# Dividing tiles 48 to 73 of a row maximum anew, and letting GpSimd find most of the last number-free rows

## Chip, cores, metric

One core of a Trainium2 chip. The metric is the device time of one execution in microseconds (us), as a median of several executions.

## The reference

```python
batch, seq, dim = 32, 2048, 2048
x = np.random.randn(batch, seq, dim).astype(np.float32)
x[np.random.rand(batch, seq, dim) < 0.1] = np.nan
return np.nanmax(x, axis=-1).astype(np.float32)     # 65536 rows of 2048; a row without numbers gives NaN
```

## The kernel before

Each of 128 partitions holds 512 rows. They are read in 74 tiles of 28 quarter rows (28Q; 1Q is 512 elements, the first tile has 4Q). Work on a tile goes through three engines: ScalarE reads the upper 16 bits of each float and writes a key in which NaN has become smaller than every number (a "read"); GpSimd, or for a part of the tile ScalarE, turns keys back into upper halves (a "write-back"); VectorE takes the maximum of each row. Each tile is described by its loads, its pieces for ScalarE's reads (a negative number is written back by ScalarE itself, a tuple is read at once and written back apart) and its reductions, all in Q:

```python
TILES = (
    [([4], [4], [4])]
    + [([28], [7, 9, 12], [16, 12])] * 7
    + [([28], [9, 12, -7], [8, 20])]
    ...                                   # this pair of lines six times: tiles 1 to 48; then 49 to 57; cut
    + [([28], [7, 9, 12], [12, 16])] * 3                    # tiles 58 to 60
    + [([28], [7, 9, 12], [16, 12])]                        # tile 61
    + [([19, 9], [12, (5, -7), 4], [12, 16])]               # tile 62
    ...                                                      # cut
    + [([5, 4, 4, 4, 3, 4, 4], [2, 3, 4, (1, -2), 2, 3, 3, 4, (-1, 3)], [4, 8, 4, 4, 4, 4])]
    + [([4, 4, 3, 2, 3, 4, 1, 2, 3, 2], [4, 4, 3, -2, 3, (3, -1), 3, (-1, 1), 2, -1], [4, 4, 4, 4, 4, 4, 4])]
)
GROUPS = [TILES[i : i + 15] for i in range(0, 60, 15)] + [TILES[60:]]
FLAGGED = (3, 4)                          # after these groups the number-free rows are found
...
                    for c in parts:
                        ...               # kp: this piece's keys, to: where they go; cut
                        if back:
                            e = act([e_key], out=to, in_=kp, func=ACT.Copy, bias=float(TOP), scale=-1.0)
                        else:
                            e = pool([e_key], out=to, in0=kp, scalar1=-1.0, scalar2=float(TOP), op0=ALU.mult, op1=ALU.add)
...
            e = dve(after, nc.vector.tensor_scalar, out=none, in0=acc, scalar1=NONE,
                    scalar2=float(0x00C00000), op0=ALU.is_equal, op1=ALU.mult)
            e = dve([e], nc.vector.tensor_tensor, out=bits, in0=bits, in1=none, op=ALU.bitwise_or)
```

A row without numbers comes out as one known value (NONE); the two last instructions find it and make NaN of it. For the last 98 rows of a partition they stand behind the very last reduction, and the store of those rows behind them.

## Time and profile before

| | before |
|---|---|
| median of 3 runs | 1253.81 us (1253.79 to 1254.08) |
| span of the profiled run | 1251.8 us |
| VectorE, ScalarE, GpSimd busy | 89%, 79%, 93% |
| HBM read | 536.87 MB, 429 GB/s over the span |
| read of the last bytes | all but stragglers by about 1242.1 us; last load landed 1242.66 us |
| last reduction ends | 1248.23 us |

The prediction shows the lines that carry this. DVE is VectorE, ACT ScalarE, POOL GpSimd, SPq the queue that issues loads and stores. In a chain of waits a line is start, length, engine and line of the kernel, "x9" is nine instructions in a row; "idle before <- releaser" in brackets, in a timeline, is how long the engine stood and what ended it. The reading of it: the read fills everything up to 1242, so the change can only touch the tail.

### The profile page before, as it was taken

The numbers are of one execution on the slowest core, as the hardware profiler recorded it, in microseconds if no ns is written. First come the engines' busy times: TensorE is split into PE (matmuls) and PEld (weight loads), VectorE is DVE, ScalarE is ACT, GpSimd is POOL, SyncE is SP. The second block draws the span as 40 slices with busy tenths as digits, with TensorE's granted clock in tenths as the row PEclk, the third lists the DMA queues.
The fourth block names the chain that finished last, engine by engine and source line by source line (L and its number), as shares of the span: only waits on it lengthen the run. The fifth ranks groups of instructions, "written<-read, shape, count | busy, mean of one in ns | idle before, by whom it ended". The sixth has DMA issues, their size and how long they took to land.

```text
span 1251.8 us, 872 instructions
## 1 busy us (share of the span) xinstructions
DVE 1110.5 (89%) x169; ACT 988.5 (79%) x271; POOL 1166.9 (93%) x239
## 2 busy tenths in 40 slices
DVE  0888989888889988898988888998888899999999
ACT  3777887778787877788777877787777878989997
POOL 2999989998999899998999899989999999999997
DMA  9999999999999999999999999999999999999997
GB/s 415 440 421 429 440 440 440 424 427 440 440 440 427 424 440 440 438 431 421 440 440 438 432 420 440 440 438 434 418 440 440 436 438 421 431 434 426 430 427 289
DMA packets 16279, 537.20 MB, mean 429 GB/s; under 512 B 2448, under 2 KB 2448, under 8 KB 3472
## 3 DMA queue, kind: packets, MB, share of 16 engines
q1 hardware_dynamic: 16272, 537.14, 99.3%
q14 instruction: 7, 0.06, 0.0%
HBM read 536.87 MB, written 0.26 MB: 429 GB/s over the span
## 4 chain that ended last, share of the span: by engine, by line
DVE 37%; DMA 35%; POOL 17%; ACT 10%; issue 1%; SPq 0%; DVEq 0%
DVE acc L194 37%; DMA xt<-in_x_dram 35%; POOL xt L190 17%; ACT kt L186 9%; ACT xt L186 1%; SPq L228 0%; DVE none L194 0%; DVEq L124 0%; SPq L384 0%; SPq L182 0%
## 5 line engine op out<-in xcount | busy, mean ns | idle before, releaser
L190 POOL TENSOR_SCALAR xt<-kt 128x3584 int16<-128x3584 uint16 (+8 forms) x235 | 1166.7, 4965 | 78.7 <-ACT kt L186 60.1
L194 DVE TENSOR_REDUCE acc<-xt 128x3 f32<-128x6144 f32 (+4 forms) x164 | 1108.8, 6807 | 137.1 <-POOL xt L190 127.7
L186 ACT ACTIVATE kt<-xt,scalars 128x3584 uint16<-128x3584 int16 (+9 forms) x248 | 936.0, 3812 | 255.8 <-DMA xt<-in_x_dram 237.9
L186 ACT ACTIVATE xt<-kt 128x3584 int16<-128x3584 uint16 (+4 forms) x21 | 53.5, 2545 | 0.7
L186 ACT ACT_TABLE_LOAD x1 | 1.3, 1283 | 0.9 <-SPq L182 0.9
L196 DVE MEMSET scalars<- 128x1 f32 x1 | 0.1, 59 | 1.0 <-SPq L182 1.0
L194 DVE TENSOR_SCALAR none<-acc 128x414 int32<-128x414 f32 (+1 forms) x2 | 0.9, 428 | 0.1
L194 DVE TENSOR_TENSOR acc<-acc,none 128x414 int32<-128x414 int32 (+1 forms) x2 | 0.8, 422 | 0.1
L370 POOL MEMSET const-float32-0.0<- 128x1 f32 x1 | 0.1, 99 | 0.2 <-issue 0.2
L186 ACT ACTIVATE scalars<-scalars 128x1 f32<-128x1 f32 x1 | 0.2, 202 | 0.0
L370 POOL MEMSET const-bfloat16-1.0<- 128x1 bf16 x1 | 0.1, 102 | 0.0
L370 POOL MEMSET const-uint8-127<- 128x1 uint8 x1 | 0.1, 102 | 0.0
L370 POOL MEMSET const-float32-1.0<- 128x1 f32 x1 | 0.1, 99 | 0.0
## 6 DMA issues: line engine op xcount, KB each, us to landing
xt<-in_x_dram SPq DMA_DIRECT2D x61, 7168.0 KB, 22.5
xt<-in_x_dram SPq DMA_DIRECT2D x12, 1024.0 KB, 27.5
xt<-in_x_dram SPq DMA_DIRECT2D x5, 2048.0 KB, 22.0
xt<-in_x_dram SPq DMA_DIRECT2D x2, 4864.0 KB, 18.9
xt<-in_x_dram SPq DMA_DIRECT2D x2, 3584.0 KB, 22.0
xt<-in_x_dram SPq DMA_DIRECT2D x3, 2304.0 KB, 20.4
xt<-in_x_dram SPq DMA_DIRECT2D x5, 1280.0 KB, 26.3
xt<-in_x_dram SPq DMA_DIRECT2D x1, 4608.0 KB, 18.5
```

What stands on the lines that cost most here:

```text
L186: return order.add("act", nc.scalar, lambda: nc.scalar.activation(**kw), deps)
L190: "pool", nc.gpsimd, lambda: nc.gpsimd.tensor_scalar(**kw), deps
L194: return order.add("dve", nc.vector, lambda: do(**kw), deps)
L196: e_top = order.add("dve", nc.vector, lambda: nc.vector.memset(top, EDGE), [])
L370: nc = _bacc.Bacc("TRN2", target_bir_lowering=False, num_devices=1)
```

## The change

Its intent is a shorter tail. First, VectorE's finding of the last rows shrinks from 98 rows to 7: the rows of tiles 60 to 72 become a group of their own, and GpSimd finds them behind its last piece. (The words of the change say two tiles; in the code one tile is left to VectorE.) The finding now multiplies by 0x00800000, and GpSimd adds the result to the bits where VectorE ORs it in; both still make a NaN of NONE. Second, tiles 48 to 73 are divided anew (51 and 56 stay as they were). Third, a write-back given as a float is held until ScalarE has issued its next read, unless it is the tile's last; so two are held, one in tile 72 and one in tile 73.

```diff
-    + [([28], [9, 12, -7], [8, 20])]                 # tile 48
-    ...
+    + [([28], [6, 10, 12], [16, 12])] * 3
+    ...                                               # tiles 51 to 60; cut
+    + [([28], [8, 11, 9], [8, 8, 12])]               # tile 61
+    + [([20, 8], [11, -6, 6, 5], [16, 12])]          # tile 62
+    ...                                               # cut
+    + [([5, 6, 5, 4, 4, 3, 1], [(-2, 3), 3, 3, (4, -1), 4, 4, -2.0, 2], [4, 4, 3, 1, 4, 4, 4, 4])]
+    + [([4, 4, 3, 2, 4, 2, 3, 3, 3], [2, 2, 4, (-2.0, 1), 2, 3, 3, (-1, 2), (1, -1, 1), 2, -1.0], [4, 4, 4, 4, 4, 4, 4])]
 )
-GROUPS = [TILES[i : i + 15] for i in range(0, 60, 15)] + [TILES[60:]]
-FLAGGED = (3, 4)
+GROUPS = [TILES[i : i + 15] for i in range(0, 60, 15)] + [TILES[60:73], TILES[73:]]
+FLAGGED = (3, 5)
+LATE = 4
...
+                    release()             # after the next read: write back what was held
                     for c in parts:
...
                         if back:
-                            e = act([e_key], out=to, in_=kp, func=ACT.Copy, ...)
+                            held.append((at - c, at, key, kp, e_key))
+                            if not wait or at == sum(loads) * Q:
+                                release()
...
+            if gi == len(GROUPS) - 1:
+                e = find("pool", nc.gpsimd, late_after, late_acc, late, ALU.add)
+                ready[LATE] = e
```

## The prediction

> **What bounds the kernel now.** I read the page first (busy shares, the forty slices), then the chain that ended last, then the operation groups by shape, then single engines and windows of 1 us near the end. Tiles are numbered from 0; every tile but the first is 28 quarter rows (28Q; a quarter is 512 elements) per partition, so 7 rows. The page:
>
> ```profile
> span 1251.8 us, 872 instructions
> DVE 1110.5 (89%) x169; ACT 988.5 (79%) x271; POOL 1166.9 (93%) x239
> DMA  9999999999999999999999999999999999999997
> GB/s 415 440 421 429 440 440 440 424 427 440 440 440 427 424 440 440 438 431 421 440 440 438 432 420 440 440 438 434 418 440 440 436 438 421 431 434 426 430 427 289
> ```
>
> No compute engine is full over the span, but DMA is full in every slice but the last: the kernel lives on one read of 536.87 MB. To be won are only the head and the tail behind the last load, and the change leaves the head alone. Windows of 1 us (stretch, length, busy us of VectorE, ScalarE, GpSimd, clock, DMA share, GB/s):
>
> ```profile
> 1240.00:1241.00 1.00, 1.00 (x1) 1.00 (x2) 1.00 (x1) 1.00 0.97 396
> 1241.00:1242.00 1.00, 1.00 (x2) 1.00 (x2) 0.69 (x2) 1.00 0.89 265
> 1242.00:1243.00 1.00, 1.00 (x1) 0.97 (x2) 1.00 (x1) 1.00 0.17 43
> 1243.00:1244.00 1.00, 1.00 (x2) 1.00 (x2) 0.92 (x2) 1.00 0.00 0
> ```
>
> The last load is in at about 1242.1. Behind it lie 9.7 us, 0.8% of the span. The chain from tile 61 on (start, us, what), cut to its two ends:
>
> ```profile
> 1037.96 3.29 ACT kt L186
> 1041.25 0.07 issue
> 1041.32 4.19 POOL xt L190
> 1045.51 0.08 issue
> 1045.59 5.34 POOL xt L190
> 1050.94 0.02 issue
> 1050.96 66.86 DVE acc L194 x9
> ...
> 1245.93 2.30 DVE acc L194
> 1248.23 0.02 issue
> 1248.25 0.27 DVE none L194
> 1248.53 0.02 issue
> 1248.55 0.26 DVE acc L194
> ```
>
> Tile 61 lands at 1037.96; ScalarE and GpSimd prepare its first 16Q; from 1050.96 VectorE never stops: 43 reductions of 91 rows in 197.3 us (to 1248.23). So the end of the tail is VectorE's, though not by much: the timeline of ScalarE shows that it, too, is full from 1229.93 on, and its last write-back starts at 1245.05 and takes 0.79, to 1245.84, just before VectorE's last reduction at 1245.93:
>
> ```profile
> 1243.29 1.73 ACT L186 ACTIVATE kt<-xt,scalars 128x1024 uint16<-128x1024 int16 x2
> 1245.05 0.79 ACT L186 ACTIVATE xt<-kt 128x512 int16<-128x512 uint16 x1
> ```
>
> **What the Trainium skill says.** ScalarE: Activation LUTs, section What ACT_TABLE_LOAD costs: an ACTIVATE with a pointer bias takes about 280 ns + 0.833 ns per element, and neighbours overlap by about 93 ns. The trace agrees for the reads (1536 elements: 1560 ns; reads of 3584 and 4608 elements, 3279 and 4122 ns apart, take 7.31 us together, 90 ns less). The write-backs are slower than that page has it (186 ns + 0.833 per element, 1465 ns at 1536, for immediate operands): 1929 ns here, which I use. GPSIMD Engine Reference, section 3.1: an add of two inputs takes about 2.6 cycles per element at 1.2 GHz, some 0.2 us for 91 elements (my estimate); no such instruction is in the trace. SBUF — State Buffer, section Who interferes with whom: tensor_reduce never contends with GpSimd on trn2. The trace agrees: one row takes 2274 to 2276 ns beside a busy GpSimd, and 2.30 us in the last with GpSimd idle. DMA: Bandwidth & Descriptors, section Where 436 GB/s comes from: a ceiling of 435 GB/s; the trace has 440 in many slices, so this read is at the ceiling and a new order of work can't hasten it.
>
> **The change part by part.**
>
> Landings. The same bytes are read in the same order. First loads of tiles 58 to 61 land 16.89 us apart (ScalarE's waits end at 987.30, 1004.18, 1021.07, 1037.96), and the queue was never dry, so tile 61 again lands at 1037.96 and the last load at about 1242.1. The pieces of the tail's loads are about as many as before, so I change nothing here.
>
> Start of VectorE's unbroken run. Durations by shape: ScalarE reads of 6Q, 8Q take 2.85, 3.70; GpSimd 6Q 3.62, 8Q 4.77, 9Q 5.34, 10Q 5.91, 11Q 6.48; about 0.08 between. Tile 60, now 6, 10, 12: its first 16Q are ready at 1021.07 + 2.85 + 0.07 + 3.62 + 0.08 + 5.91 = 1033.6, reduced by 1048.8 (15.15 for a tile). Tile 61, now 8, 11, 9 with reductions of 2, 2 and 3 rows: GpSimd ends the pieces at 1037.96 + 3.70 + 0.07 + 4.77 = 1046.5, 1053.06 and 1058.5. VectorE: 1048.8 to 1053.2, to 1057.6, waits 0.9, 1058.5 to 1065.1. Before, tile 61 was done at 1050.96 + 15.2 = 1066.15: 1.05 us gained.
>
> VectorE's work after it. From 2276 ns for one row and 8686 for four: (8686 - 2276)/3 = 2.137 us per row and 0.14 per instruction, of which about 0.08 overlaps with the one before (8.69 + 6.55 against 15.15 for a pair), leaving 0.06. Check on before: 91 x 2.137 + 43 x 0.06 = 197.0, measured 197.3. Tiles 62 to 73 had 41 reductions and get 52 (2, 3, 3, 2, 3, 3, 5, 5, 4, 7, 8, 7): 11 x 0.06 = 0.7 us more. New end of the last reduction: 1065.1 + 84 x 2.137 + 52 x 0.06 = 1247.7, if it never waits; before, 1248.2. Net gain about 0.4, allowing 0.1 us of idle time.
>
> ScalarE and GpSimd. Over tiles 61 to 73 write-backs rise from 15 of 44Q to 19 of 49Q. From the durations by shape I sum 197.7 us for ScalarE (194.6 before) and 191.6 for GpSimd (194.5 before), against 204.2 us from tile 61's landing to the last. ScalarE's 3.1 us go into waits (the view of waits gives it 8.1 us on reads and 1.7 on GpSimd from 1050 on before). The two pieces marked as held write back behind the next read: the gap of 0.03 between a read and its own write-back becomes an overlap of about 0.1, so 0.13 each, 0.3 us in all, already in that sum.
>
> Last tile on ScalarE. It can begin at about 1227.5, when its first 4Q are in (1225.03, seen at the end of a wait, plus 4 x 0.61). Eleven reads: 11 x 0.28 + 28 x 0.428 = 15.1; write-backs of 2, 1, 1 and 1Q: 1.35 + 3 x 0.78 = 3.7; overlaps less gaps -1.2: 17.6 us, to 1245.1, against 1245.84 before. The floor from the last landing is 1242.1 + 1.13 + 0.7 + 0.8 = 1244.7. So ScalarE frees the last row 0.7 us sooner, and that is no longer what holds the end: VectorE gets to it at 1247.7 - 2.28 = 1245.4.
>
> Finding the number-free rows. VectorE's two instructions shrink from 98 elements to 7 (the code leaves one tile, not two, to the last group). From 593 ns at 414 elements and 264 at 98: 1.04 ns each, so 91 fewer spare 2 x 0.095 = 0.19 us on the path. GpSimd's two instructions on 91 elements, an estimate of 0.3 us each from its fixed 0.2 us and the above, start when its last piece is done, about 1244.8, and end near 1245.5 beside VectorE's last reductions: hidden. One store more, ready about two us ahead of the last: hidden too. The last store's 3.5 KB should take the 1.7 us of the 49 KB one.
>
> Sum: 0.4 + 0.2 = 0.6 us off 1253.81: 1253.2.
>
> **The rivals.** First, new waits on VectorE: with 52 reductions cut to fit the pieces, each waits for one piece, and ScalarE is 3 us fuller. For it speaks that a walk by hand over tiles 62 to 67 leaves margins of only 0 to 2 us between a piece being ready and VectorE asking for it; against it, that a late piece in the middle is no loss unless VectorE ends later than ScalarE allows. It would cost 0.5 to 1.5 us: 1253.7 to 1254.7. Second, VectorE gains more and the last landing binds: 1244.8 + 0.1 + 2.28 + 0.35 = 1247.5 for the end of the finding against 1248.81 now, so 1252.5; nothing can go below this unless the read gets faster. For it speaks that ScalarE is so near it. Third, without the write-back of tile 48 on ScalarE (9, 12, -7 gave way to 6, 10, 12) twenty tiles run with 16.6 us of GpSimd work against 16.9 us of reading, and 16.7 where the slices show 440 GB/s. GpSimd could fall behind by some 0.1 us per tile there, but slices of 420 give it back, and the tiles from 49 to 61 ran so before. I give it under 0.5 us. Fourth, the finding on GpSimd or its store ends last: it has about 2 us of room, so it would have to take four times my estimate; then up to +1 us.
>
> **Range and chances.** The middle is 1253.2. Floor 1252.5, less 0.5 for another read rate: 1252.0. Above, waits of the first rival and a little of the third: 1254.6. A gain of 2% is 25 us, nearly three times all that lies behind the last load; a loss of 2% would need a new wait of about 1.8 us in each of the last 14 tiles, with nothing to absorb it. Faster 0.01, same 0.98, slower 0.01.
>
> **What would show it.** Right: DMA full until about 1242; VectorE's chain unbroken from about 1058.5; its last reduction ending near 1247.7; the last finding two instructions of about 0.17 us on 7 elements; ScalarE's last write-back done near 1245.1; GpSimd's two instructions over by 1246. Wrong: if VectorE shows idle time behind ScalarE or GpSimd between 1060 and 1245, if the reads end elsewhere than at 1242, or if the store of the 91 rows is what the end waits for.

## The result, and the profile after

The change takes 1253.68 us (median of 6 runs, 1253.59 to 1253.85) against 1253.89 us for the kernel before in the same rounds (6 runs, 1253.76 to 1254.15). The ratio is the mean time of one kernel's fast runs over that of the other's of the same rounds, so not quite the ratio of the medians: 0.9998, 95% interval 0.9985 to 1.0011. That is the same within 2%, and 0.2 us lower in the medians.

From the page of the changed kernel (its span is 1251.8 us, as before):

```profile
DVE 1110.9 (89%) x181; ACT 986.9 (79%) x273; POOL 1168.4 (93%) x242
DMA  9999999999999999999999999999999999999997
```

The DMA row is as before. The windows of 1 us show the bulk of the read ending where it did (264 and 53 GB/s in the two windows where before had 265 and 43), but stragglers of the last load land later: it was complete at 1243.20 instead of 1242.66.

```profile
1241.00:1242.00 1.00, 1.00 (x1) 1.00 (x2) 0.92 (x2) 1.00 0.88 264
1242.00:1243.00 1.00, 1.00 (x2) 1.00 (x1) 1.00 (x1) 1.00 0.19 53
```

The chain that ended last, cut to tile 61 and the last rows, without its "issue" lines of 0.02 to 0.08 us:

```profile
1038.12 8.60 ACT kt L187 x2
1046.79 6.48 POOL xt L191
1053.35 5.35 POOL xt L191
1058.72 6.55 DVE acc L195
...
1213.18 23.03 DMA xt<-in_x_dram
1236.24 1.58 ACT kt L187
1237.89 1.92 POOL xt L191
1239.84 2.01 DVE acc L195
...
1246.42 2.29 DVE acc L195
1248.74 0.18 DVE none L201
1248.94 0.16 DVE acc L215
```

Two things are to be seen. Tile 61 went as worked out: done at 1058.72 + 6.55 = 1065.27, 27.15 us after its landing, where before needed 28.15. But the chain no longer runs through VectorE alone: it goes back from the fourth-last reduction over GpSimd and ScalarE to a load of the last tile that landed at 1236.21, and the last reduction ends at 1248.71, not earlier than before but 0.48 us later. The timeline around it:

```profile
1233.78 1.15 ACT L187 ACTIVATE kt<-xt,scalars 128x1024 uint16<-128x1024 int16 x1 [0.33 <-DMA xt<-in_x_dram]
1237.89 8.42 POOL L191 TENSOR_SCALAR xt<-kt 128x1536 int16<-128x1536 uint16 x6 [0.95 <-ACT kt L187]
1239.84 8.87 DVE L195 TENSOR_REDUCE acc<-xt 128x1 f32<-128x2048 f32 x4 [0.50 <-POOL xt L191]
1245.54 0.77 ACT L187 ACTIVATE xt<-kt 128x512 int16<-128x512 uint16 x1
1246.40 0.55 POOL L201 TENSOR_SCALAR late<-acc 128x91 int32<-128x91 f32 x1
1247.03 0.34 POOL L215 TENSOR_TENSOR acc<-acc,late 128x91 int32<-128x91 int32 x1
```

GpSimd stood 0.95 us and VectorE 0.50 us behind that read of ScalarE's. The load itself left ScalarE idle for only 0.07 us, the load before it for 0.33 us (first line), so the chain's last step names the smaller of two waits for the read. ScalarE and GpSimd both end their last piece at 1246.31, and GpSimd's finding (0.55 and 0.34 us) is over at 1247.37, hidden.

Laid side by side, the two spans agree, in four terms: tile 61 landed 0.16 us later (1038.12 against 1037.96); from there to the end of the last reduction it took 210.59 instead of 210.27 us (+0.32); the finding on VectorE 0.39 instead of 0.58 (-0.19); and from there to the end of the span 2.70 instead of 2.97 us (-0.27), of which most is the last store: the one of 3.5 KB landed in 1.40 us, the one of 49 KB in 1.66. The sum is 0.02. So the finding and the small store gained about half a microsecond, and the new tail gave most of it back.

The second term is the steadier measure: the end of the last reduction less the landing of tile 61 (the moment at which ScalarE's wait for it ends). Times of whole runs of one kernel differ by up to 0.9 us, and over the traces tile 61 lands anywhere from 1037.92 to 1038.58 us, whichever kernel it is; this "tail length" of one kernel's traces agrees within 0.13 us.

### The profile page after: what moved, and what is told of

Same layout as the page of the kernel before. It is cut to its first block, busy times and chain, and to the rows that moved or that the text cites. A ratio compares the mean times of both kernels' runs of the same rounds, so it can differ in the third digit from the quotient of the medians.

```text
span 1251.8 us, 892 instructions
## 1 busy us (share of the span) xinstructions
DVE 1110.9 (89%) x181; ACT 986.9 (79%) x273; POOL 1168.4 (93%) x242
## 4 chain that ended last, share of the span: by engine, by line
DMA 36%; DVE 33%; POOL 19%; ACT 10%; SPq 1%; issue 1%; DVEq 0%
DMA xt<-in_x_dram 36%; DVE acc L195 33%; POOL xt L191 19%; ACT kt L187 9%; ACT xt L187 1%; SPq L253 1%; DVE none L201 0%; DVE acc L215 0%; SPq L411 0%; DVEq L124 0%; SPq L183 0%
## 5 line engine op out<-in xcount | busy, mean ns | idle before, releaser
L191 POOL TENSOR_SCALAR xt<-kt 128x3584 int16<-128x3584 uint16 (+11 forms) x236 | 1167.4, 4946 | 78.5 <-ACT kt L187 60.3
L187 ACT ACTIVATE xt<-kt 128x512 int16<-128x512 uint16 (+6 forms) x24 | 52.8, 2200 | 0.7
```

The source lines that it names most:

```text
L187: return order.add("act", nc.scalar, lambda: nc.scalar.activation(**kw), deps)
L191: "pool", nc.gpsimd, lambda: nc.gpsimd.tensor_scalar(**kw), deps
```

## The experiments

All were correct. "Before" is the kernel before in the same rounds. Medians are of 5 runs (4 where said), of before 9.

**Which half gained: the finding alone.** Before's tiles, the change's finding and its groups.

```diff
 # the change, with
-TILES = ...  # the change's
+TILES = ...  # before's
```

> The tiles of before with the new finding alone (13 tiles' rows on GpSimd, 7 rows on VectorE). Theory A (the two halves of the change pull apart: the finding gains, the tiles lose): the last reduction ends as before, near 1248.2; the finding takes 0.35 instead of 0.55 us; the small last store lands 0.3 us sooner than the 49 KB one; so about 0.5 us faster than before (1253.4) and 0.3 faster than the change. Theory B (the finding on GpSimd gains nothing, the 0.2 us are the tiles'): as before, 1253.9.

Measured: 1253.56 us, before 1253.93; ratio 0.9998 (0.9984 to 1.0012). The tail is before's to the hundredth, 1248.24 - 1037.97 = 210.27. Its last lines in the timeline:

```profile
1248.26 0.17 DVE L203 TENSOR_SCALAR none<-acc 128x7 int32<-128x7 f32 x1
1248.47 0.16 DVE L217 TENSOR_TENSOR acc<-acc,none 128x7 int32<-128x7 int32 x1
```

The expectation of Theory A is met in its direction (0.37 us below before, 0.5 expected; the change, in other rounds, was 0.21 below); the store's part did not show in this trace (1.7 us to landing). Repeated on another chip:

> The tiles of before with the new finding again, on another chip: 0.3 to 0.4 us below before if that gain is real, 210.27 us from tile 61's landing within 0.05, and the small last store 0.25 us quicker from its issue than the 49 KB one (the first trace of it did not show that).

Measured: 1253.52 us, before 1253.90 (ratio 0.9998, 0.9984 to 1.0012). Tail 210.18, 0.04 beyond what I allowed. The store landed in 1.54 us, 0.12 quicker than the large one and not 0.25. Twice 0.37 or 0.38 us below before in the median, so the gain is as steady as this measure allows, though the interval of the ratio does not part it from zero. No kernel is further below before; it was never run in the same rounds as the change, so that it beats the change rests on two comparisons with before. Measured in the traces from tile 61's landing to the end of the span, it gains 0.18 and 0.40 us.

**The other half: the tiles alone.** The change with before's finding of 98 rows on VectorE.

```diff
-GROUPS = [...] + [TILES[60:73], TILES[73:]]
+GROUPS = [...] + [TILES[60:]]
-FLAGGED = (3, 5)
+FLAGGED = (3, 4)
```

> The new tiles with the old finding (98 rows on VectorE at the end, one 49 KB store). Theory A: the last reduction ends at about 1248.7, 0.5 us later than before, and nothing makes it good: about 0.4 to 0.5 us slower than before, 1254.3. Theory B (the tiles are what gained): 0.2 us faster than before, 1253.7.

Measured: 1254.17 us, before 1253.93; ratio 1.0003 (0.999 to 1.0015). Tail 210.61. Theory A holds in its direction: the new tiles lose 0.2 to 0.3 us (0.4 to 0.5 expected).

**Tiles 48 to 60.** Before, with only these divided as in the change; and the counterpart, the change with before's tiles 0 to 60.

```diff
-    + [([28], [9, 12, -7], [8, 20])]
-    + [([28], [7, 9, 12], [16, 12])] * 4 ...
+    + [([28], [6, 10, 12], [16, 12])] * 3 ...        # tiles 48 to 60 only
```

> Before, with only tiles 48 to 60 divided as in the change (no write-back on ScalarE in tile 48). If GpSimd falls behind without that relief (third rival): first reduction of tile 61 later than 1051.0 and the end later by the same, up to 0.5 us. If not: tile 61 still waits for its landing, the last reduction ends at 1248.2 within 0.2, time as before within 0.2 us.

Measured: 1254.42 us, all five runs above 1254.2, before 1253.93; ratio 1.0004 (0.9991 to 1.0016). Tile 61 landed at 1038.40, 0.44 later than in the trace of before, and its first reduction was 13.26 us after that (1051.66; before 13.00), so 0.26 of lag; but the tail was 210.33, and the lag was gone at the end.

> Tiles 0 to 60 of before, tiles 61 to 73 and the finding of the change. The part alone of tiles 48 to 60 cost 0.49 us in the earlier run. Theory A (that cost is carried into the change): this is 0.3 to 0.5 us faster than the change. Theory B (the new tail absorbs GpSimd's lag, because tile 61 begins with a small reduction): same as the change within 0.15 us.

Measured: 1253.52 us (1253.47 to 1254.1), before 1253.67; ratio 1.0 (0.9987 to 1.0012). Tail 210.62. The change itself took 1253.52 in these rounds. Theory B: tiles 48 to 60 cost the change nothing. The 0.49 us of the first run do not lie in these tiles by its trace: it is 0.96 us longer than that of before, 0.44 by the later landing and 0.47 behind the finding, where the large store took 1.93 us to land instead of 1.66. Over all traces, kernels with before's tiles 48 to 60 land tile 61 at 1037.96, 1037.97, 1038.32, 1038.33 and 1038.58, those with the new ones at 1037.92 to 1038.58 (nine traces, median 1038.31): no difference. Why that one kernel was slow in all five runs stays open.

**The change again**.

> The change itself, word for word, on the chip of the other three. It gives what one chip and the next differ by, and a second trace: if the last loads and tile 61's landing move by 0.2 to 0.4 us between two traces of one kernel, differences of that size in a single trace are the read's, not the change's. Expected: 0.2 us below before, within 0.15; last reduction again held by ScalarE's read behind the fifth load of the last tile (0.4 to 0.6 us idle on VectorE near 1239.8).

Measured: 1253.52 us, before 1253.67; ratio 0.9999 (0.9985 to 1.0012): 0.15 us lower. The tail is 210.72 us, the same wait is there:

```profile
1239.78 8.86 DVE L195 TENSOR_REDUCE acc<-xt 128x1 f32<-128x2048 f32 x4 [0.48 <-POOL xt L191]
```

**Does VectorE's time bind?** The change, with the finding of the 91 rows moved from GpSimd to VectorE, between the last two tiles.

```diff
-FLAGGED = (3, 5)
-LATE = 4
+FLAGGED = (3, 4, 5)      # and no finding on GpSimd
```

> The change, but VectorE itself finds the rows of tiles 60 to 72 between the last reduction of tile 72 and the first of tile 73, about 0.55 us of VectorE time; GpSimd finds nothing. If VectorE's rows bind without a break (my prediction's reading): 0.5 us slower than the change. If VectorE is held by the last tile's landing and ScalarE (it waited 0.5 us at 1239.8 in the change's trace): the 0.55 us fall into that wait and the time is that of the change within 0.15 us.

Measured: 1253.78 us, before 1253.93; ratio 0.9999 (0.9986 to 1.0011). Tail 210.66, with 0.52 us more work on VectorE in the chain:

```profile
1232.88 0.27 DVE none L199
1233.16 0.25 DVE acc L213
```

VectorE's rows do not bind without a break: the work fell into its wait. It also shows that GpSimd was not needed for this gain; done on VectorE ahead of the last tile it cost no more, within the 0.13 us by which tails of one kernel differ.

**Is it the fifth load?** The chain of the change pointed to the load of quarters 13 to 17 in the last tile, of which ScalarE wants the first three. The change with that load cut smaller, and the write-back in front of the wait not held (two edits at once).

```diff
-    + [([4, 4, 3, 2, 4, 2, 3, 3, 3], [2, 2, 4, (-2.0, 1), 2, ...
+    + [([4, 4, 3, 2, 3, 3, 3, 3, 3], [2, 2, 4, (-2, 1), 2, ...
```

> The change, with the last tile's loads of 4 and 2 quarters cut as 3 and 3 and the first held write-back of that tile done at once. Theory A (the end hangs on the landing of the fifth load, which ScalarE's read of rows 13 to 16Q waits for; at 0.61 us per quarter it then comes 0.6 us sooner): last reduction 0.4 to 0.5 us sooner, time 0.4 us below the change. Theory B (VectorE's rows bind, the idle 0.5 us is given back elsewhere): no change within 0.15 us.

Measured: 1253.52 us, as the change in these rounds (1253.52); ratio to before 1.0 (0.9987 to 1.0012). Tail 210.56. The wait for that load is gone, but:

```profile
1237.23 11.34 DVE L195 TENSOR_REDUCE acc<-xt 128x1 f32<-128x2048 f32 x5 [0.19 <-POOL xt L191]
1239.15 1.57 ACT L187 ACTIVATE kt<-xt,scalars 128x1536 uint16<-128x1536 int16 x1 [0.20 <-DMA xt<-in_x_dram]
```

Five reductions follow one another, starting after a wait of 0.19, and end where they did; ScalarE waits for a later load, the seventh. Theory B's time came, but not for its reason that VectorE's rows bind. The chain that ended last in this run, cut:

```profile
1217.72 21.41 DMA xt<-in_x_dram
1239.15 1.58 ACT kt L187
...
1244.83 1.36 POOL xt L191
1246.28 2.30 DVE acc L195
```

From the landing of the seventh load, at 1239.13, ScalarE's four reads and three write-backs take 7.05 us; with them, at 1246.18, GpSimd's last piece is done, and VectorE's last reduction starts 0.10 us later, 2.38 us after the one before it instead of the usual 2.19. In the change the same path had the same length (1239.26 to 1246.31, the last reduction at 1246.42), and VectorE's own rows came out level with it. So the run relieved one of two equal paths, and removing the wait was worth at most 0.16 us.

**Holding write-backs.** The change with none held.

```diff
-4, 4, -2.0, 2]   ...   (-2.0, 1), 2, 3, 3   ...   2, -1.0]
+4, 4, -2, 2]     ...   (-2, 1), 2, 3, 3     ...   2, -1]
```

> The change without holding any write-back behind the next read. My prediction: two held write-backs are worth 0.13 us each on ScalarE, 0.3 us in all, so if ScalarE's work in the last tile sets the end this is 0.1 to 0.3 us slower. If the landing of the fifth load sets it, ScalarE waits for that load anyway (it had idle 0.33 us before it): same within 0.15 us.

Measured: 1253.96 us, before 1253.67, the change 1253.52; ratio 1.0002 (0.999 to 1.0015). Tail 211.07, 0.35 to 0.48 longer than the change's two.

```profile
1225.98 1.34 ACT L187 ACTIVATE xt<-kt 128x1024 int16<-128x1024 uint16 x1
1228.53 2.19 ACT L187 ACTIVATE kt<-xt,scalars 128x1024 uint16<-128x1024 int16 x2 [0.21 <-DMA xt<-in_x_dram]
1235.62 2.29 DVE L195 TENSOR_REDUCE acc<-xt 128x1 f32<-128x2048 f32 x1 [0.47 <-POOL xt L191]
1238.32 11.06 DVE L195 TENSOR_REDUCE acc<-xt 128x1 f32<-128x2048 f32 x5 [0.42 <-POOL xt L191]
```

The write-back at 1225.98 now stands ahead of the last read of tile 72, so GpSimd's next piece comes later; VectorE stands twice, 0.89 us. Holding is worth about 0.4 us here (0.44 by the medians of these rounds, where 0.1 to 0.3 or nothing was expected). That it is by what comes first rather than by overlap (0.13 us each) is the reading of one trace, and not shown apart: in it the first three loads of tile 73 also landed 0.8 us later after tile 61 than in the change, and ScalarE waited 0.21 us for one of them (second line) and 0.31 us for another.

**About one microsecond more on ScalarE, or on GpSimd.** The change with two dummy instructions ahead of tile 72 (they read old results and write to scratch).

```diff
+                if number == 73:
+                    for i in range(2):
+                        act([], out=extra[:, i * 384 : i * 384 + 384], in_=accs[:, :384], func=ACT.Copy)
```

> The change with two dummy copies of 384 elements on ScalarE ahead of tile 72, about 0.95 us of extra work there. Measured from tile 61's landing to the end of the last reduction (210.6 to 210.7 us in every run of the change's tail). Theory A (ScalarE sets the end of the last tile): it had 0.4 us of idle time left in tile 73, so the end moves by 0.4 to 0.6 us. Theory B (VectorE's rows bind, ScalarE has room): the end moves by less than 0.2 us.

Measured (4 runs): 1254.03 us, before 1253.90; ratio 1.0 (0.9987 to 1.0014). ScalarE was held for 0.83 us (1211.23 to 1212.06), the tail stayed at 1249.14 - 1038.55 = 210.59. In the profiled run the later end is all later landing. Theory B by its letter, but ScalarE's room is not shown cleanly: in this trace the seventh load of the last tile landed 200.79 us after tile 61, against 201.15 and 201.28 in the change's two, so ScalarE waited less for the read; and VectorE stood 0.22 us at 1223.89, where it had not. For GpSimd, two of 320 elements:

> The change with two dummy instructions of 320 elements on GpSimd ahead of tile 72, 1 to 1.6 us of extra work. Theory A (GpSimd only follows ScalarE; it had 0.95 us idle at 1237): the end moves by less than 0.3 us. Theory B (GpSimd is as tight as the others before that gap): VectorE gets its rows of tile 72 later and the end moves by 0.5 us or more.

Measured (4 runs): 1254.29 us, before 1253.90; ratio 1.0003 (0.9989 to 1.0016). For 0.96 us on GpSimd (1214.62 to 1215.58) the tail grew to 210.94, by 0.22 to 0.35, with VectorE standing here:

```profile
1224.11 25.25 DVE L196 TENSOR_REDUCE acc<-xt 128x1 f32<-128x513 f32 x12 [0.45 <-POOL xt L192]
```

Between the two theories: most of it went into GpSimd's 0.95 us of idle time, a third or a quarter came through (with the seventh load at 200.88, again sooner than in the change, so rather too little than too much).

**A version meant to beat both.** Before's tiles and the new finding, with tile 61 as in the change and two held write-backs.

```diff
-    + [([28], [7, 9, 12], [16, 12])]
+    + [([28], [8, 11, 9], [8, 8, 12])]
-[4, 4, 3, -2, 3, (3, -1), 3, (-1, 1), 2, -1]
+[4, 4, 3, -2.0, 3, (3, -1.0), 3, (-1, 1), 2, -1]
```

> A version meant to beat both: the tiles of before, but tile 61 as in the change, two held write-backs in the last tile, and the new finding. If VectorE's start and ScalarE's work both bind in the old tail, their relief together ends it 0.2 to 0.4 us sooner than the finding alone did (210.27 us from tile 61's landing becomes 209.9 to 210.1). If holding makes VectorE wait for the held quarters, 210.3 or more.

Measured: 1254.20 us, before 1253.90; ratio 1.0002 (0.9989 to 1.0014). A miss: tail 210.83, 0.6 longer than with the finding alone.

```profile
1238.10 11.06 DVE L197 TENSOR_REDUCE acc<-xt 128x1 f32<-128x2048 f32 x5 [0.53 <-ACT xt L189]
```

VectorE had to wait for the held quarters themselves. It also stood 0.58 us at 1066.08 and 0.24 at 1081.47, in tiles 62 and 63, behind GpSimd: most of the 0.98 us that the new tile 61 gained was lost there at once, because the pieces of before's next tiles were not ready sooner. Holding frees ScalarE's next read and delays its own rows; here the rows were wanted at once.

The tails of all traces, in us from tile 61's landing to the end of the last reduction:

| tail | traces |
|---|---|
| before's last tiles | 210.27 (before), 210.27 and 210.18 (finding alone), 210.33 (with new tiles 48 to 60) |
| the change's last tiles | 210.59, 210.72 (the change), 210.61 (old finding), 210.66 (early finding on VectorE), 210.62 (old tiles before), 210.56 (other loads), 210.59 (more on ScalarE) |
| longer | 210.94 (more on GpSimd), 211.07 (nothing held), 210.83 (mixed) |

## Why the prediction was right or wrong

The time (1253.68 for 1253.2) lies in the range and the verdict is the predicted one, but of the 0.6 us gain 0.2 came, and of its two terms one had the wrong sign. That 0.2 us are left is luck in part: the store's quarter of a microsecond, which the prediction did not count, and the loss in the tiles nearly cancel; and "same" would have come with any of the tails measured here.

- **The read ends at 1242 and bounds the gain**: right for the bulk of the bytes. The landing of the last load was read too early off the windows: 1242.66 before, and 1243.20 in the change. ScalarE's read of it began 0.57 us after that, so it did not hold the end.
- **Tile 61 and VectorE's start**: right. 27.15 us after its landing, worked out 1065.1 - 1037.96 = 27.1. Only the landing itself was 0.16 later; taking it as fixed to the hundredth was wrong, since it moves by up to 0.66 us between traces.
- **VectorE's work after it**, the step that failed: the last reduction at 1247.7, with 0.1 us of idle time allowed. From the end of tile 61 (1065.27) it took 183.44 us instead of the 182.6 of the sum (84 x 2.137 + 52 x 0.06). Of the 0.8 us missing, 0.50 are the wait at 1239.84, the rest is work: 183.44 - 0.50 - 84 x 2.137 = 3.4, so 0.066 per reduction where I had 0.06 (the prediction's check on before had left 0.3 us over in the same way). Against the tail of before this makes +0.32 instead of -0.4.
- **The last tile on ScalarE**, 1245.1 predicted and 1246.31 measured, is the step behind it: it began at 1227.84, not 1227.5, behind the held write-back of tile 72 (+0.3); it waited 0.4 for loads where I had let none interfere; and its instructions took 18.07 us, not 17.6, because I had counted an overlap at pairs that did not have one (+0.5). The same error runs through the whole tail: 194.6 and 197.7 us summed for ScalarE, 197.5 and 200.6 us busy in the traces, though the difference is right. The conclusion that ScalarE no longer holds the end fell with it: its last write-back ends 0.11 us before VectorE's last reduction starts, and in eight of the nine traces with these tiles it ends 7.04 to 7.06 us after the seventh load's landing.
- **First rival** (new waits on VectorE, 0.5 to 1.5 us): this is what happened, at 0.5 us, and I had made it a rival though my walk stopped at tile 67 and never reached the last two tiles, where the wait is. **Third rival** (GpSimd falls behind without tile 48's relief): 0.26 us of lag at tile 61 with before's last tiles, none at the end. **Fourth** (the finding on GpSimd or its store ends last): no; it was over at 1247.37, 1.34 us ahead of the last reduction's end, though it took 0.89 us for my 0.6 and began at 1246.40 for my 1244.8.
- **Finding**: right, 0.19 us worked out and measured. **The store**, "should take the 1.7 us of the 49 KB one": mis-sized; in the change's trace it landed in 1.4 us, and from the end of the finding to the end of the span it takes 2.70 to 2.97 us in the eleven traces with the small store, 2.90, 2.97 and 3.44 in three of the large one. About a quarter of a microsecond of the change's gain is from there. Size alone does not tell: the small store took 1.40 us in all eight traces with the change's last tiles, and 1.54, 1.54 and 1.67 with before's.
- **Held write-backs**, 0.3 us by overlap: nearly right in size (0.35 to 0.48 in the tail). The reason was probably another, that the next read, and so GpSimd's next piece, comes sooner; that is not shown apart from later loads in that trace.

What binds the new tail is not one engine. In six of the nine traces with its tiles (the change twice, the old finding, the early finding, the old tiles before, the other loads) the last reduction ends 9.43 to 9.46 us after the landing of the last tile's seventh load: 7.05 us of ScalarE, 0.1 us, and a reduction of 2.28. VectorE's rows behind the fifth load come out level with that in the change, so relieving them alone, by the other loads, gained nothing, and 0.52 us more on VectorE cost nothing while it still had a wait. Where it ends later than that (more on ScalarE, more on GpSimd, nothing held) VectorE had stood before. This is read from the traces' landings; no run took work from ScalarE behind the seventh load, so what that would gain stays open.

## What to carry to other kernels

Work at the very end that depends on the last result should be cut to what only the last result needs: the 7-row finding and its small store gave nearly 0.4 us by the medians (0.18 and 0.40 us in two traces). Where several engines and the read are level in the last tile, a chain of waits names one of them truly, and relieving that one alone may gain nothing, as it did here: look for the path that comes out level with it. Time won early in the tail (0.98 us at tile 61) is kept only if the tiles after it are ready sooner too. To judge tenths of a microsecond, measure from a common event (here the landing of one tile) rather than from the start of the run, and compare where the later loads landed as well: against tile 61 the seventh load of the last tile moved by up to 0.49 us between traces with the change's last tiles.

## What the Trainium skill lacked or had wrong

- ScalarE: Activation LUTs, What ACT_TABLE_LOAD costs: 0.833 ns per element for every ACTIVATE. The write-backs, whose 16-bit results go to every second place, take 1.11 ns per element (781 ns at 512 elements, 4199 at 3584); the reads, which take every second place and write without gaps, agree with the page. Nor does it say that the overlap of 93 ns is lost where the second instruction waits for the first: a write-back behind its own read starts 0.04 us after that read's end (1239.34 and 1239.38 in the kernel before).
- GPSIMD Engine Reference, section 3.1: no figure for the whole fixed cost of a small instruction (section 2.1 has only tens of cycles for one call in the dispatch). 91 elements took 343 ns for the integer add and 545 ns for compare and multiply (f32 to int32), although 320 elements of multiply and add (f32 to 16 bits) took 458 ns.
- DMA: Bandwidth & Descriptors, Where 436 GB/s comes from: a ceiling of 435 GB/s. Many fortieths of the span show 440.
